# Two table splits of an expert loop computed on VectorE instead of GpSimd

## The chip, the cores and the metric

The kernel runs on one core of one Trainium2 chip. The metric is the device time of one execution in microseconds (us). The engines are named as in the profile: PE is TensorE's matrix multiplies, PEld its loads of weights, DVE is VectorE, ACT is ScalarE, POOL is GpSimd and SP is SyncE, which here only issues transfers.

## The reference, cut to what matters

The program is a whole network: two hybrid layers, a second block with attention and a recurrent branch, and at the end a layer of experts (`peer_ffn`), in which the change lies. Each of 512 tokens (1024 features) has 8 heads, and each head picks 16 of 16384 experts, by the best sums of two scores over 128 keys each. Expert e has a row of 1024 numbers in a first table `peer_u` and one in a second table `peer_v`.

```python
N_KEYS = 128; N_EXPERTS = N_KEYS * N_KEYS; PEER_HEADS = 8; PEER_TOPK = 16

def one_chunk(xc):                       # 128 tokens
    ...                                  # scores, top_s and eidx: the 16 best of each head
    gate = jax.nn.softmax(top_s, axis=-1)
    act = jax.nn.gelu(jnp.einsum('chkd,cd->chk', peer_u[eidx], xc))
    return jnp.einsum('chk,chkd->cd', (gate * act).astype(xc.dtype), peer_v[eidx])
```

## The kernel before

**Two ways for the tokens.** `peer` treats the four tiles of 128 tokens in two ways. Three of them (384 tokens) meet all 16384 experts: products of the tokens with the whole first table, gelu, multiplication by a matrix of gates that is zero where an expert was not chosen, and products with the whole second table. The fourth tile gathers its own experts: for each token one row of a table at a time, 128 times for the first table and 128 times for the second (`gathered`).

**The loop over the experts** (L2343) runs i from -7 to 127. A step takes 128 experts, and works on several of them at once: PE makes the products `u` of the first table for expert tile i+5 (24 matmuls, 384 columns each) and the products `acc` with the second table for tile i (18 matmuls, 512 columns each). For tiles 6 to 33 the first product was made earlier and is read back from DRAM (`xd`), so PE has the `u` part only from i = 29 on.

**High and low parts.** A table tile comes as 128x1024 fp32 (`raw`, 512 KB). `halves` (L2337) splits it into two fp32r tiles: ACT rounds it to the high part (`v<-raw` or `u<-raw`, a CAST), and another engine subtracts to get the low part (`v<-raw,v` or `u<-raw,u`, a TENSOR_TENSOR with two inputs in SBUF). PE makes three products for each pair of operands from them. There are 128 such tiles of the second table in the loop and 94 of the first one (from tile 34 on; the earlier ones are split elsewhere, and are not touched). The second table's tile is split two steps ahead of its use, for i+2, the first one's seven steps ahead, for i+7, and that is two steps before its product.

**What VectorE does in a step**, in its order: `x<-gq,x` and `x<-x,W` (gelu's second half and the gates, for tile i+3), `gq<-gq,x` (gelu's first half, tile i+4), `al<-x,ah` (low part of the gated activations, tile i+1), for even i the low part of the second table's tile, and then the fourth token tile's work. Up to i = 38 that is one step of its routing (top 16 and so on); after that it is about three gathered rows in a step, a dot product each (`pr<-gr,H`, L2577) while the first table is gathered, and a multiply-add each (`pr<-gr,gq,pr`, L2584) with the second.

**What GpSimd does in a step:** for odd i the low part of the second table's tile, from i = 27 on the low part of the first table's tile in every step, and from i = 39 on about three gathers (L2563, DMA_INDIRECT), each of which it issues itself.

**What sets the order.** In this loop PE, DVE, ACT and POOL execute in the order in which the program is written: `Core` wraps every engine, and its helper (L63) pins each instruction. So L63 is the line of nearly all of them, and rows are told apart by tile names. SP's loads are ordered by a scheduler. `raw` tiles come from a ring of 6 that a step takes two of; a load can start when the low part that read the slot before it is done. Gathered rows `gr` have a ring of 7 and are used 4 gathers after they are asked for (LAG). Tiles `u` and `v` have rings of 3, `ah` and `al` of 2.

Of the kernel before, what the change touches and what calls it, by code (L numbers as in the profile page):

```python
# [54 lines left out]
class Pinned:  # L55
    """An engine with its instructions in the order they are written in."""
# [9 lines left out]
class Core:  # L66
    """All engines so."""
# [7 lines left out]
class Feed:  # L75
    """Weights in the order of their use, 512 columns a tile, loaded ahead and split into two parts that one pass each carries."""

    def __init__(self, net, raw, split):
        self.net, self.nraw, self.nsplit = net, raw, split
        self.src, self.raws, self.tiles, self.over = [], [], {}, set()  # L80
        self.taken = self.dead = 0
        # another pool for what is loaded before weight number last
        self.more, self.last = None, 0

    def add(self, w, r0, c0, n, order=None, both=False):
        """1024 rows of n columns; returns the number of row tiles in a tile."""
        kt = min(KD, T // n)
        for rows in order or [range(k, k + kt) for k in range(0, KD, kt)]:
            self.src.append((w, r0 + rows[0] * P, rows[1] - rows[0], kt, c0, n, both))
        return kt  # L90
# [39 lines left out]
def part(gen, n):  # L130
    """The next n steps of a generator."""
    for _ in range(n):
        if next(gen, gen) is gen:
            return
        yield
# [7 lines left out]
def among(a, b, n):  # L143
    """A generator with n steps of another one after each of its own."""
    for _ in a:
        yield
        yield from part(b, n)


def weave(ticks, *work):  # L150
    """Steps of several generators in turn: (generator or (function, its argument), from, to, number of steps)."""
# [12 lines left out]
def tables():  # L164
    """Constants of shapes alone, [128, n] each: for all of the program, for block 1, for block 2."""
# [20 lines left out]
    # axial rotation, token major: [128, token tile, 64]  # L186
# [23 lines left out]
class Net:  # L210
# [34 lines left out]
    def row(self, ap, n, pool=None, tag=None):  # L245
        """A DRAM row of n on all partitions."""
# [4 lines left out]
    def wtile(self, w, r0, c0, n):  # L251
        """128 rows of a weight, split into two parts that one pass each carries."""
# [16 lines left out]
    def rstd(self, out, ss, n, eps=1e-6, nc=None):  # L269
        """out = (ss / n + eps) ** -0.5"""  # L270
# [12 lines left out]
    def defer(self, n, f, *x):  # L283
        """f, n steps of the projections later."""
# [12 lines left out]
    def unit_t(self, w, c0, x, evac, n=P, tok=slice(0, T)):  # L297
        """Eight steps to a block of columns of a product, transposed: evac(psum [n, tokens])."""
# [19 lines left out]
    def unit_n(self, w, r0, c0, x, evac, pairs=(0, 1), order=((0, 1), (2, 3), (4, 5), (6, 7))):  # L318
        """Eight steps to 256 columns of a product of each pair of token tiles: evac(pair, psum [tokens, 2, 256])."""
# [23 lines left out]
    def norm_pair(self, p, g, x, pool, s=1):  # L343
        """Two token tiles of X, normed, to columns of the transposed operand: staged, s steps for each stage."""
# [36 lines left out]
    def layer(self, l, S):  # L381
        """The layers of block 1 in two parts: the order of what meets the weights; the work. The heads run on a plan of
        ticks, 24 for a head of the first kind (M) and 12 for one of the second (B), and projections are woven in."""
# [13 lines left out]
        # ---- what follows the projections  # L397
# [49 lines left out]
        def rope(nm, b):  # L447
            """Rotated queries or keys of two heads, split as the products of scores take them."""
# [57 lines left out]
        # ---- the order of the weights  # L506
# [34 lines left out]
        # ---- the heads  # L541
# [5 lines left out]
        def pofs(d, i, t):  # L547
            """Column of key tile i, query tile t among the kept blocks."""
# [89 lines left out]
        def turned(n, src, k):  # L638
            """128 columns of a mixed output, transposed and split."""
# [67 lines left out]
        # ---- the work  # L707
# [69 lines left out]
    def norms(self, name, g, S):  # L777
        """What the staged norm of the two pairs of token tiles takes, and a new transposed operand."""
# [5 lines left out]
    def block1(self):  # L784
        tc, nc, a = self.tc, self.nc, self.a
        with ExitStack() as st:
            # on the way into block 2: the transposed operand, and until then X
# [8 lines left out]
            # the table of functions, before data is there  # L796
# [30 lines left out]
    def final_part(self, p, s, k):  # L827
        """X times the final gain, 256 columns of a pair of token tiles, and their sums of squares before and after."""
# [11 lines left out]
    def final_rest(self, p, xs, mod, bank, x, s, n0):  # L840
        """X = rms_norm(X, final_g) of two token tiles; normed once more, scaled and shifted per feature, to columns of
        the transposed operand. Staged, s steps for each stage."""
# [52 lines left out]
    def gates(self, l, ps, q, tl):  # L895
        """The gates of block 1 from their sums: staged."""
# [85 lines left out]
    def ahead(self, S):  # L982
        """What block 2 takes from its conditions and its context alone."""
# [16 lines left out]
    def block2_params(self, pool):  # L1000
# [16 lines left out]
        # lambda, the same on all partitions  # L1017
# [11 lines left out]
    def attn_params(self, cp):  # L1029
        nc, a = self.nc, self.a  # L1030
        self.load_tables(2, cp)
        # gains of q and k folded into the rotation
# [24 lines left out]
    def mods(self, pool):  # L1057
        """Modulation vectors: per feature columns, and rows for the two that gate a residual."""
# [48 lines left out]
    def modulated_xt(self, tiles, s1, sh, xh, xl, pool, bank, back=None, first=0, to=None):  # L1107
        """Normalised token tiles -> split transposed operand, scaled and shifted per feature, or as it is to DRAM."""
# [21 lines left out]
    def normed_of(self, src, pool, out=None):  # L1130
        """src / rms, in a tile of the pool or over src."""
# [10 lines left out]
    def block2(self):  # L1142
# [17 lines left out]
        # the operands of the projections again as places for others: of [128, T], high and low  # L1160
# [26 lines left out]
    def attention(self):  # L1187
        """Differential attention, a quarter (two heads) at a time; while the heads of one quarter run, the
        projections of the next are woven in. Yields once before x is needed, with the function that gives
        banks, and once before the last quarter, whose fill it is sent."""  # L1190
# [5 lines left out]
        with ExitStack() as left:  # L1196
# [8 lines left out]
            def loads():  # L1205
                """256 columns of the weight at a time, split in two: four tiles of two row tiles each."""
# [26 lines left out]
            def bank_of(i, xh, xl, b, evac, last=False):  # L1233
                """Projection i of two token tiles to 256 columns."""
# [14 lines left out]
            def headed(nm, q, o, rotate, last):  # L1249
                """Queries or keys of two token tiles: normed by heads, rotated, and split as the products take them."""  # L1250
# [52 lines left out]
            def ahead(u):  # L1303
                """What a quarter takes from the context: keys and values."""
# [37 lines left out]
            def scores(n):  # L1342
                """Products of queries and keys, and their exponentials: 4 ticks for each of a unit's four maps."""
# [28 lines left out]
            def turned(u):  # L1372
                """A quarter's outputs, transposed."""
# [16 lines left out]
            def outs(n, x):  # L1390
                """The difference of a unit's maps, transposed, and its product with the values."""
# [91 lines left out]
    def wblock(self):  # L1483
        """The next two row tiles of a block of 128 columns, of weights laid [128, block, 8, 128], split in two; others are asked for ahead."""
# [14 lines left out]
    def rwkv(self, hxh, hxl, hch, hcl, mmt2, bank2, lead):  # L1499
        """Delta-rule heads by chunks of 64 tokens, a block of 128 channels (two heads) at a time, both  # L1500
        directions together and in three groups: 4 chunks of context, then 4 and 4 of x. While the chain
        over the chunks of one group runs, the inverses of the next, the decays of the one after it and
        the projections of the next block are woven in."""
# [7 lines left out]
        with ExitStack() as st:  # L1511
# [12 lines left out]
            # what no chain takes: gives way to the work that fills the last ones  # L1524
# [21 lines left out]
            def proj(b, dst, both=True):  # L1546
                """Shifted channels of block b, of context and x."""
# [18 lines left out]
            def block(ct, o):  # L1566
                """Projections, unit keys, bonus of a block of channels."""
# [9 lines left out]
                # unit keys, times -1/2  # L1577
# [25 lines left out]
            def tail(o):  # L1603
                """Bonus and values of a block of channels."""
                k, r, v, ct = o["k"], o["r"], o["v"], o["ct"]
                # bonus
                rk = tl([P, T], "rk")
                nc.vector.scalar_tensor_tensor(rk, r, self.rk_[:, ct:ct + 1], k[:, C:], op0=ALU.mult, op1=ALU.mult)
                # values, token major
# [15 lines left out]
            def pairs(j):  # L1625
                """The first of the group's two pairs of chunks, for each direction."""
                return ((0, 0), (2, 4), (4, 2))[j]

            def decays(o, g):
                """Decays and rates of a group, and its keys and receptances with the decays on them."""  # L1630
# [33 lines left out]
                # slots of a chunk pair: k even, b even, b odd, k odd; r even, kk even, kk odd, r odd  # L1664
# [15 lines left out]
            def products(o, g):  # L1680
                """Products within the chunks of a group, in both directions."""
# [4 lines left out]
                for d in range(2):  # L1686
# [17 lines left out]
                    # keys and rates, token major, stacked as the values are  # L1704
# [8 lines left out]
            def values(o, g):  # L1713
                """Values over and under zeros, for what is found of the rates."""
# [8 lines left out]
            def newton(x):  # L1723
# [16 lines left out]
                def keep(ps, Z):  # L1740
                    """Into the diagonal blocks that the steps of the chain take."""
# [9 lines left out]
            def chain(o, g):  # L1751
                """The state over the four chunks of a group, and what the receptances read of it."""
# [81 lines left out]
            def gate(b):  # L1834
                """A block of the merge gates, to DRAM: work that fills the tensor engine."""
# [22 lines left out]
            def branch_in(src, ks, at):  # L1858
                """Rows of a branch's outputs, split."""
# [20 lines left out]
            def branch(b, ks, at, evac, *src):  # L1880
                """A block of a branch's product."""
# [16 lines left out]
            def gated_b(b, ps, g, f):  # L1898
                """Of the branches merged by their gates all but what the last block of the second one brings."""
# [4 lines left out]
            # where no operand stands any more when the second branch is under way  # L1904
# [757 lines left out]
```

## Time and profile before

| what | value |
|---|---|
| median of 3 runs | 4966.08 us |
| lowest and highest run | 4948.15 and 4974.35 us |
| span of the profiled execution | 4986.3 us |
| PE busy in it | 4530.2 us, 91% |
| DVE busy | 3463.8 us, 69% |
| ACT busy | 1993.8 us, 40% |
| POOL busy | 2156.0 us, 43% |

The profiled execution is known by its span alone, 4986.3 us from its first to its last instruction; that is 20 us (0.4%) above the median of the timed runs. A busy share is a mean over the whole network. The loop over the experts takes the stretch from about 3870 us to the end, and shares of that stretch are read from views of it. An instruction's time in a row begins when its engine takes it up; an engine that has started an instruction but cannot go on shows a long instruction, not an idle gap.

### The profile page before, as it was taken

What the parts mean: (1) busy time and instruction counts of PE and PEld (TensorE: products, weight loads), DVE (VectorE), ACT (ScalarE), POOL (GpSimd) and SP (SyncE); (2) the same over time, 40 slices, a digit from 0 to 9 for tenths busy, and PEclk for the clock granted to TensorE, in tenths of its full rate; (3) what the DMA queues carried; (4) which work ended last, traced back from release to release, by engine and by line L of the source; (5) the groups of instructions that cost most, each with busy time, mean ns of one, the idle gap of its engine ahead of it and who ended that gap; (6) DMA issues with size and microseconds to landing.
All of it is one profiled execution on the core that took longest, in us unless ns stands there. A gap on an engine that the chain in (4) does not pass through costs nothing. (4 is left out here: it accounts for less than half of the span.)

```text
span 4986.3 us, 78323 instructions
## 1 busy us (share of the span) xinstructions
PE 4530.2 (91%) x29167; PEld 3864.4 (78%) x29167; DVE 3463.8 (69%) x6705; ACT 1993.8 (40%) x4288; POOL 2156.0 (43%) x1715
## 2 busy tenths in 40 slices
PE   8999999999998998888898889889799889988987
PEld 6789897888888886677776767768677678877776
DVE  4654234655656654677777877668753989999999
ACT  3444334443325554344444444433222444333333
POOL 3324443324434332322232333144433247888886
PEclk8999999999999999788788888999678999999999
DMA  4234333235653211000000001462344447887886
GB/s 128 72 86 133 96 115 98 69 89 157 189 186 112 55 46 42 19 21 18 20 21 23 23 26 36 134 213 92 104 125 153 158 160 274 294 289 278 289 291 230
DMA packets 435687, 618.46 MB, mean 124 GB/s; under 512 B 32596, under 2 KB 318436, under 8 KB 435176
## 3 DMA queue, kind: packets, MB, share of 16 engines
q1 hardware_dynamic: 392104, 469.87, 30.0%
q0 software_dynamic: 36864, 134.23, 7.8%
q10 hardware_dynamic: 6336, 9.35, 0.6%
q8 instruction: 229, 3.75, 0.3%
q14 instruction: 154, 1.26, 0.1%
HBM read 549.36 MB, written 48.24 MB: 120 GB/s over the span
## 5 line engine op out<-in xcount | busy, mean ns | idle before, releaser
L63 POOL TENSOR_TENSOR wlo<-wraw,whi 128x512 fp32r<-128x512 f32 x451 | 614.9, 1369 | 897.3 <-ACT whi L63 850.6
L63 ACT CAST whi<-wraw 128x512 fp32r<-128x512 f32 x572 | 347.3, 617 | 564.4 <-PE mm L63 369.8
L63 PE MATMUL acc<-v,ah 128*128 128x512 f32 x1536 | 444.7, 414 | 4.3 <-ACT ah L63 4.3
L1495 POOL TENSOR_TENSOR wbl<-wblk,wbh 128x256 fp32r<-128x256 f32 (+1 forms) x184 | 148.3, 806 | 615.4 <-ACT wbh L1494 362.9
L63 PE MATMUL u<-hph,u 128*128 128x384 f32 x1504 | 400.6, 338 | 4.5 <-ACT x L63 4.5
L63 PE MATMUL mm<-whi,u 128*128 128x256 f32 x2048 | 377.2, 285 | 4.5 <-ACT u L63 2.7
L63 PE MATMUL acc<-v,al 128*128 128x512 f32 x768 | 264.2, 427 | 113.1 <-DVE al L63 112.8
L63 PEld LDWEIGHTS acc<-v,ah 128*128 128x128 f32 x1536 | 309.0, 202 | 68.0 <-ACT ah L63 4.6
L63 PE MATMUL mm<-xh,whi 128*128 128x512 f32 (+2 forms) x880 | 342.8, 390 | 8.0 <-ACT r L63 4.6
L63 PE MATMUL mm<-xh,wlo 128*128 128x512 f32 (+2 forms) x880 | 328.9, 374 | 0.0
L63 PEld LDWEIGHTS mm<-whi,u 128*128 128x128 f32 x2048 | 323.4, 193 | 6.5 <-ACT u L63 3.3
L63 PE MATMUL mm<-xl,whi 128*128 128x512 f32 (+2 forms) x880 | 328.4, 373 | 0.0
L63 POOL TENSOR_TENSOR u<-raw,u 128x1024 fp32r<-128x1024 f32 x94 | 273.3, 2908 | 81.0 <-ACT u L63 80.8
L63 ACT ACTIVATE gq<-gq 128x384 f32<-128x384 f32 x128 | 67.1, 524 | 595.4 <-DVE gq L63 595.4
L63 PE MATMUL mm<-wlo,u 128*128 128x256 f32 x1024 | 291.6, 285 | 5.0 <-POOL wlo L63 4.6
L63 PEld LDWEIGHTS acc<-v,al 128*128 128x128 f32 x768 | 151.5, 205 | 169.4 <-DVE al L63 140.4
L63 PEld LDWEIGHTS u<-hph,u 128*128 128x128 f32 x1504 | 275.4, 189 | 9.1 <-ACT x L63 4.9
L63 DVE SCALAR_TENSOR_TENSOR x<-gq,x 128x384 f32<-128x384 f32 x128 | 264.6, 2067 | 12.9 <-ACT gq L63 12.2
L63 POOL TENSOR_TENSOR v<-raw,v 128x1024 fp32r<-128x1024 f32 x64 | 195.1, 3048 | 171.7 <-ACT v L63 159.6
L63 PE MATMUL u<-hpl,u 128*128 128x384 f32 x752 | 253.5, 337 | 0.0
L63 PE MATMUL mm<-whi,xh 128*128 128x256 f32 x768 | 236.0, 307 | 0.0
L63 PE MATMUL mm<-whi,xl 128*128 128x256 f32 x768 | 219.5, 286 | 0.1
(608 smaller groups left out, 13232.8 us busy)
## 6 DMA issues: line engine op xcount, KB each, us to landing
raw<-in_ut_dram SPq DMA_DIRECT2D x128, 512.0 KB
raw<-in_peer_v_dram SPq DMA_DIRECT2D x128, 512.0 KB
wraw<-in_w_in_dram SPq DMA_DIRECT2D x184, 256.0 KB
wraw<-in_w_down_dram SPq DMA_DIRECT2D x160, 256.0 KB
wraw<-in_w_up_dram SPq DMA_DIRECT2D x152, 256.0 KB
mraw<-in_w_mod_dram SPq DMA_DIRECT2D x96, 256.0 KB
wg<-stage SPq DMA_DIRECT2D x12, 2048.0 KB
W<-wg SPq DMA_DIRECT2D x32, 768.0 KB
```

What stands on the lines that cost most here:

```text
L63: return lambda *a, **k: self.tc.keep_in_program_order(f(*a, **k))
L1495: (nc.vector if self.wn > WN and n % 2 else nc.gpsimd).tensor_tensor(lo, raw, hi.bitcast(F32), op=ALU.subtract)
```

## The change

Both calls of `halves` in the loop name VectorE as the engine that subtracts. For the second table that moves 64 of 128 low parts, those of odd i, and for the first table all 94. The computation, the tiles, their rings and all other instructions stay. The diff also empties docstrings and comments in the file, without moving a line; those hunks are left out.

```diff
@@ -2385,9 +2385,9 @@
                 if 0 <= i + 2 < P:
-                    halves(i + 2, "v", gp, k.gpsimd if i % 2 else k.vector)
+                    halves(i + 2, "v", gp, k.vector)
                 if NA <= i + 7 < P:
-                    halves(i + 7, "u", wp, k.gpsimd)
+                    halves(i + 7, "u", wp, k.vector)
```

First place: VectorE, two steps of the loop while rows of the first table are gathered, before the change. `gr` are gathered rows; the second step here has no low part of a table at all.

```order
 L63 TENSOR_TENSOR v_43796<-raw_43600,v_43795 128x1024
 L2577 ISA pr_43288,act_43287<-gr_43673,H 128x1024
...
 L63 SCALAR_TENSOR_TENSOR x_43786<-gq_43788,x_43786 128x384
 L63 TENSOR_TENSOR x_43786<-x_43786,W_43450 128x384
 L63 SCALAR_TENSOR_TENSOR gq_43864<-gq_43864,x_43862 128x384
 L63 TENSOR_TENSOR al_43868<-x_43632,ah_43867 128x384
 L2577 ISA pr_43288,act_43287<-gr_43749,H 128x1024
```

The same two steps on VectorE after the change:

```order
 L63 TENSOR_TENSOR v_43796<-raw_43600,v_43795 128x1024
 L63 TENSOR_TENSOR u_43800<-raw_43602,u_43799 128x1024
 L2577 ISA pr_43288,act_43287<-gr_43673,H 128x1024
...
 L63 SCALAR_TENSOR_TENSOR x_43786<-gq_43788,x_43786 128x384
 L63 TENSOR_TENSOR x_43786<-x_43786,W_43450 128x384
 L63 SCALAR_TENSOR_TENSOR gq_43864<-gq_43864,x_43862 128x384
 L63 TENSOR_TENSOR al_43868<-x_43632,ah_43867 128x384
 L63 TENSOR_TENSOR v_43872<-raw_43676,v_43871 128x1024
 L63 TENSOR_TENSOR u_43876<-raw_43678,u_43875 128x1024
 L2577 ISA pr_43288,act_43287<-gr_43749,H 128x1024
```

Each step now has both low parts between `al` and the first dot product.

Second place: GpSimd in the same steps, the difference of its order from before to after.

```order
-L63 TENSOR_TENSOR u_43800<-raw_43602,u_43799 128x1024
 L2563 DMA gr_43821<-in_peer_u_dram,ei_43211 128x1024
 L2563 DMA gr_43824<-in_peer_u_dram,ei_43211 128x1024
 L2563 DMA gr_43827<-in_peer_u_dram,ei_43211 128x1024
-L63 TENSOR_TENSOR v_43872<-raw_43676,v_43871 128x1024
-L63 TENSOR_TENSOR u_43876<-raw_43678,u_43875 128x1024
 L2563 DMA gr_43897<-in_peer_u_dram,ei_43211 128x1024
 L2563 DMA gr_43900<-in_peer_u_dram,ei_43211 128x1024
```

Three subtractions in two steps are gone from GpSimd, and only the gathers are left on it here. The order on PE and ACT is the same before and after. On SP a few loads trade places before i = 27, a read of `xd` with the load of `peer_v` next to it; the later loads keep their order.

## Rows read from the trace of the kernel before

**Rows 1.** The page, the chain of work that ended last, shares by line.

```profile
DVE x L63 5%; DVE pr L2584 3%; DVE pr L2577 2%; PE acc L2535 2%; PE acc L2536 2%; DVE gq L63 1%; PE acc L63 1%; DVE al L63 1%; DVE v L63 1%; PE u L63 1%; PE u L267 1%; PE u L266 1%; PE u L265 1%; DVE sel L2489 0%; DVE pz L2479 0%
```

**Rows 2.** Busy us by stretch: PE, PEld, DVE, ACT, POOL; then clock, DMA share, GB/s.

```profile
3900.00:4000.00 100.00, 82.55 (x324) 64.08 (x324) 97.25 (x220) 41.88 (x73) 26.65 (x11) 0.93 0.52 170
4054.00:4131.00 77.00, 76.62 (x381) 69.70 (x382) 61.05 (x56) 37.72 (x60) 37.30 (x15) 0.98 0.47 154
4205.00:4546.00 341.00, 305.44 (x1443) 269.61 (x1442) 337.26 (x372) 126.60 (x204) 279.05 (x159) 0.94 0.82 291
...
4296.00:4304.00 8.00, 8.00 (x43) 7.31 (x41) 7.90 (x8) 1.39 (x2) 7.35 (x4) 1.00 1.02 419
```

**Rows 3.** Timeline of VectorE, two steps: start us, us, engine, line, operation.

```profile
4281.38 2.73 DVE L63 SCALAR_TENSOR_TENSOR x<-gq,x 128x384 f32<-128x384 f32 x1
...
4289.52 2.73 DVE L63 SCALAR_TENSOR_TENSOR x<-gq,x 128x384 f32<-128x384 f32 x1
...
4293.99 1.22 DVE L63 TENSOR_TENSOR v<-raw,v 128x1024 fp32r<-128x1024 f32 x1
4295.12 1.22 DVE L2577 CUSTOM_DVE_ANT_0 pr<-gr,H 128x1024 f32<-128x1024 f32 x1
...
4297.65 3.29 DVE L2577 CUSTOM_DVE_ANT_0 pr<-gr,H 128x1024 f32<-128x1024 f32 x1
...
4300.88 2.75 DVE L63 SCALAR_TENSOR_TENSOR x<-gq,x 128x384 f32<-128x384 f32 x1
```

**Rows 4.** Timeline of GpSimd, the same two steps.

```profile
4280.34 3.36 POOL L63 TENSOR_TENSOR u<-raw,u 128x1024 fp32r<-128x1024 f32 x1
...
4286.57 1.30 POOL L2563 DMA_INDIRECT gr<-in_peer_u_dram,ei  x1 [0.31 <-issue]
4289.31 2.52 POOL L63 TENSOR_TENSOR u<-raw,u 128x1024 fp32r<-128x1024 f32 x1 [1.44 <-ACT u L63]
...
4296.52 3.35 POOL L63 TENSOR_TENSOR v<-raw,v 128x1024 fp32r<-128x1024 f32 x1 [0.50 <-ACT v L63]
```

**Rows 5.** Timeline of VectorE while the second table is gathered: `x` at three places.

```profile
4698.50 2.74 DVE L63 SCALAR_TENSOR_TENSOR x<-gq,x 128x384 f32<-128x384 f32 x1
...
4718.29 2.75 DVE L63 SCALAR_TENSOR_TENSOR x<-gq,x 128x384 f32<-128x384 f32 x1
...
4937.19 0.55 DVE L63 SCALAR_TENSOR_TENSOR x<-gq,x 128x384 f32<-128x384 f32 x1
```

**Rows 6.** VectorE's groups, 4143.7 to 4969 us: busy us, mean ns, idle before.

```profile
L2584 DVE SCALAR_TENSOR_TENSOR pr<-gr,gq,pr 128x1024 f32<-128x1024 f32 x127 | 211.5, 1665 | 4.3 <-DMA gr<-in_peer_v_dram,ei 1.4
L63 DVE SCALAR_TENSOR_TENSOR x<-gq,x 128x384 f32<-128x384 f32 x83 | 210.2, 2533 | 0.0
L2577 DVE CUSTOM_DVE_ANT_0 pr<-gr,H 128x1024 f32<-128x1024 f32 x126 | 195.6, 1552 | 3.0
```

**Rows 7.** GpSimd's groups, 4143.7 to 4969 us.

```profile
L63 POOL TENSOR_TENSOR u<-raw,u 128x1024 fp32r<-128x1024 f32 x80 | 237.2, 2965 | 57.5 <-ACT u L63 57.3
...
L63 POOL TENSOR_TENSOR v<-raw,v 128x1024 fp32r<-128x1024 f32 x43 | 142.9, 3323 | 29.6 <-ACT v L63 21.2 <-issue 8.4
```

**Rows 8.** GpSimd's groups, 3870 to 4054 us.

```profile
L63 POOL TENSOR_TENSOR v<-raw,v 128x1024 fp32r<-128x1024 f32 x16 | 40.0, 2498 | 121.2 <-ACT v L63 117.5 <-DVE v L63 3.6
...
L63 POOL TENSOR_TENSOR u<-raw,u 128x1024 fp32r<-128x1024 f32 x3 | 7.8, 2584 | 4.5 <-ACT u L63 4.5
```

**Rows 9.** The chain that ended last, two pieces of it: start us, us, what.

```profile
4059.46 4.17 PE u L63 x24
4063.62 4.08 PE acc L63 x18
```

**Rows 10.** Timeline of PE, a wait and what follows it.

```profile
4207.91 0.72 PE L63 MATMUL acc<-v,al 128*128 128x512 f32 x2 [2.72 <-DVE al L63]
4208.47 1.71 PE L63 MATMUL acc<-v,ah 128*128 128x512 f32 x4
```

**Rows 11.** All gathers of the second table: lowest, median and highest ns of one.

```profile
L2563 POOL DMA_INDIRECT gr<-in_peer_v_dram,ei x128: 958/1098/2006, 4540.3 to 4951.7; - x128
```

## The prediction

> **What bounds the kernel now.** I read the chain that ended last first, then busy time by stretch, then the timelines of VectorE and GpSimd over the same two steps. The chain's shares [rows 1] are led by VectorE's work in the expert loop: `x`, and `pr` of both gatherings. By stretch [rows 2] the loop has three parts. From 3900 to 4000 us VectorE is busy 97.25 of 100 us and PE 82.55. From 4054 to 4131 us PE is busy 76.62 of 77 us and VectorE 61.05: PE is the bound. From 4205 us to nearly the end VectorE is busy 337.26 of 341 us, PE 305.44 at a clock of 0.94, and the transfers run at 291 GB/s with a share of 0.82. So VectorE sets the pace before 4054 us and after 4143.7 us, where the first dot products are under way.
>
> But a busy VectorE isn't a working one. `x` takes 2.73 to 2.75 us in rows 3 and 0.55 us at 4937.19 us [rows 5], with the same shape; `pr` takes 3.29 us at 4297.65 us and 1.22 us at 4295.12 us. Each long one meets a subtraction on GpSimd [rows 4]: the `u` of 4289.31 us ends at 4291.83 us, and the `x` begun at 4289.52 us ends 0.42 us later, about its own length less what overlaps. The `v` of 4296.52 us starts beside a `pr` and takes 3.35 us; the next `pr` has to wait for it. At 4937.19 us, with no subtraction on GpSimd, `x` is short. The gathers that GpSimd issues (1.30 us at 4286.57 us) lie beside instructions of VectorE that keep their 1.22 us. So VectorE stands still while GpSimd subtracts, and not while it issues gathers.
>
> The Trainium skill (SBUF — State Buffer, section "SBUF: two separate sides") says that VectorE, with two inputs in SBUF, and GpSimd take turns on one port pair, each for a whole instruction; the trace agrees (3.29 us in place of 1.22). A rule of it speaks against this change: Perfetto Trace Analysis, section "Optimizing Scalar/DVE Operations", says that offloading between these two might not help, because of that port. By it the sum below would be zero; its rival has a chance of its own.
>
> **The change part by part.**
>
> *What goes.* In the two steps from 4281.38 to 4300.88 us (19.50 us) GpSimd subtracts three times, and VectorE loses (2.73 - 0.55) + (3.29 - 1.22) + (2.75 - 0.55) = 6.45 us, 2.15 us for each [rows 3, 5]. Over the whole main stretch [rows 6]: `x` 83 x (2.53 - 0.55) = 164 us; dot products 126 x (1.55 - 1.22) = 42 us; multiply-adds 127 x (1.665 - 1.27) = 50 us, where 1.27 is the dot's 1.22 plus a sixth of the 0.29 us by which two steps are longer there (4718.29 - 4698.50 = 19.79 us [rows 5]). Together 256 us, against 80 + 43 = 123 subtractions [rows 7]: 2.08 us each. I take 2.1 us.
>
> *What comes.* The same subtraction on VectorE, for even i, is 1.22 us long, and the next instruction starts 1.13 us after it [rows 3]. So one that moves gives VectorE 2.1 - 1.13 = 0.97 us.
>
> *Main stretch.* 123 x 0.97 = 119 us, if VectorE stays the bound. Two steps then take 19.50 - 3 x 0.97 = 16.6 us, and 16.9 us with multiply-adds. The next one late is PE: `u` 4.17 us and `acc` 4.08 us at full clock [rows 9], so 16.5 us for two steps. The two are nearly equal, and this is all that the change can bring: PE's floor for the stretch is 80 x 8.25 + 6 x 4.08 = 684 us (six last steps without `u`) of 825 us, a gain of 141 us at most.
>
> *Early part.* Before 4054 us 16 + 3 = 19 subtractions move [rows 8], worth at most 19 x 0.97 = 18 us. VectorE isn't quite always the bound there; I take 15 us. The 16 between 4054 and 4143.7 us (158 in all less 123 and 19) bring nothing: PE sets the pace, and VectorE's 61 of 77 us leave room for them.
>
> *Waits that the change adds.* On VectorE the low parts wait for ACT's high parts, with the dot products and the next `x` queued behind. GpSimd takes up the `v` of 4296.52 us right after ACT's cast; VectorE's place for it is behind the `x` of 4300.88 us and three more instructions. So it has over 4 us in hand, and this wait costs nothing as long as ACT is a step ahead; if it were not, a whole cast would be lost per step. `al`, for which PE waits, stands before the low parts and isn't delayed by them. The slots of `raw` come free by VectorE's subtraction in place of GpSimd's; SP's loads behind have about two steps to land. SP's few exchanged loads before i = 27 change no load's size, and I cost them at nothing: each trades one place with a neighbour, and these steps use 0.52 of the transfers' time. On GpSimd the gathers are no longer queued behind subtractions and can only start earlier.
>
> *Sum.* 119 + 15 = 134 us. For two engines with nearly equal cycles, where each waits for the other's jitter, I take 4 us off. So 130 us: 4986.3 - 130 = 4856 us for the profiled span. The span is 20 us above the median of the runs; the gain lies in a loop whose steps repeat, so I take it off the median: 4966 - 130 = **4836 us**.
>
> **The rivals.**
>
> *Transfers become the bound.* Each step moves 291 GB/s x 9.75 us = 2.84 MB; at 8.3 us that is 342 GB/s, and the share would be 0.82 x 9.75 / 8.3 = 0.96. For it: the present bursts fill the queues only now and then. Against it: from 4296 to 4304 us 419 GB/s were moved at a full share [rows 2], and loads come more evenly when all low parts are in one place. If the mean share can't pass 0.90, a step takes 8.9 us, and with 9.8 us before, 80 x 0.9 + 15 = 87 us are gained: 4879 us.
>
> *PE becomes the bound at less than its full clock.* After a wait of 2.72 us four matmuls take 1.71 us [rows 10] where 4 x 4.08 / 18 = 0.91 us is usual: half speed, that is 1.2 for 2.4 GHz. If PE's waits for `al` get short but stay, with the mean clock at 0.94 [rows 2], a step takes 8.25 / 0.94 = 8.8 us: 80 x 1.0 + 15 = 95 us, 4871 us. Against it: from 4054 to 4131 us PE ran without waits at 0.98.
>
> *Gathers starve (slower).* GpSimd writes what the gathers need while VectorE now runs two-input instructions without a pause. An issue is 1.1 us in the median and 2.01 at most [rows 11], with 0.31 us between two [rows 4]. Three of them fill a step of 8.3 us from 2.5 us each, and the kernel gets slower than before from 2.95 us each. Had each to wait out two subtractions, 1.1 + 2.26 + 0.3 = 3.7 us, a step would take 11 us: 85 x 1.2 - 15 = 87 us slower, 5053 us. Against it: in rows 4 gathers were issued beside a VectorE that never paused.
>
> [...]
>
> *One for one.* VectorE would lose as much by the low parts as by standing still; 4966 us. Rows 3 speak against it (1.13 against 2.15 us).
>
> *The long `x` has another cause* that stays, and the low parts come on top: 142 x 1.13 = 160 us, 5126 us.
>
> **How the numbers follow.** Forecast 0.73, transfers 0.10, PE's clock 0.09, gathers 0.04, one for one 0.02, another cause 0.02. About 0.5% (25 us) is what a measurement of this kernel can tell from no change. The first three are faster by more than that: 0.92. Within it lies one for one: 0.02. Slower are the last and the starved gathers: 0.06. The range goes from 141 + 18 us (PE's floor and all of the early part), 4807 us, to a little above the transfers' case, 4888 us, since the timed runs spread by 26 us.
>
> **What would show it.** `x` at 0.55 us and `pr` at 1.22 us throughout; 128 `v` and 94 `u` low parts on VectorE at 1.22 us; two steps of 16.5 to 17 us; PE near 95 of 100 us or more at a clock near 1; gathers still near 1.1 us. I am wrong if `x` stays long, if an issue of a gather passes 2.5 us, or if VectorE or ACT waits for `raw` or `gr` step after step.

## Result and profile after

The changed kernel takes 4816.41 us in the median (4 runs, 4805.59 to 4831.27) against 4969.55 us for the kernel before (4 runs, 4948.15 to 4974.35): ratio 0.9696, 95% interval 0.9662 to 0.9731, so 3% faster, by 153 us. The forecast was 4836 us, with a range from 4807 to 4888 us.

The profiled execution spans 4816.9 us. First VectorE over two steps, where [rows 3] showed the kernel before (timeline: start us, us, engine, line, operation):

```profile
4273.14 0.55 DVE L63 SCALAR_TENSOR_TENSOR x<-gq,x 128x384 f32<-128x384 f32 x1
...
4275.44 1.22 DVE L63 TENSOR_TENSOR v<-raw,v 128x1024 fp32r<-128x1024 f32 x1
4276.58 1.22 DVE L63 TENSOR_TENSOR u<-raw,u 128x1024 fp32r<-128x1024 f32 x1
4277.72 1.22 DVE L2577 CUSTOM_DVE_ANT_0 pr<-gr,H 128x1024 f32<-128x1024 f32 x1
...
4281.39 0.55 DVE L63 SCALAR_TENSOR_TENSOR x<-gq,x 128x384 f32<-128x384 f32 x1
...
4289.65 0.55 DVE L63 SCALAR_TENSOR_TENSOR x<-gq,x 128x384 f32<-128x384 f32 x1
```

`x` is 0.55 us in each of these steps instead of 2.73 us, and no `pr` of the loop is long (1.23 and 1.29 us at most). The two low parts stand behind each other at 1.14 us. A step takes 8.26 us, two 16.51 us, where two took 19.50 us.

GpSimd in the second of these steps, for [rows 4]:

```profile
4279.21 1.80 POOL L2563 DMA_INDIRECT gr<-in_peer_u_dram,ei  x1 [3.80 <-DVE act L2577]
4281.31 0.96 POOL L2563 DMA_INDIRECT gr<-in_peer_u_dram,ei  x1 [0.30 <-issue]
4282.58 1.09 POOL L2563 DMA_INDIRECT gr<-in_peer_u_dram,ei  x1 [0.31 <-issue]
```

Only gathers are left, and GpSimd now waits 3.8 us in a step until VectorE has used a gathered row.

Busy time by stretch after the change, for [rows 2] (PE, PEld, DVE, ACT, POOL; then clock, DMA share, GB/s):

```profile
3848.70:4000.00 151.30, 132.90 (x522) 102.50 (x523) 146.83 (x365) 69.42 (x119) 4.48 (x2) 0.94 0.54 173
4000.00:4095.00 95.00, 94.77 (x485) 86.61 (x484) 72.77 (x101) 46.07 (x73) 13.61 (x9) 1.00 0.60 204
4095.00:4440.00 345.00, 345.00 (x1758) 315.50 (x1757) 339.50 (x502) 160.92 (x245) 161.88 (x126) 1.00 0.95 341
4440.00:4627.00 187.00, 187.00 (x954) 170.91 (x953) 183.92 (x205) 88.17 (x140) 90.22 (x68) 1.00 0.94 334
4627.00:4795.00 168.00, 162.41 (x809) 146.28 (x808) 165.87 (x181) 71.30 (x116) 74.46 (x57) 0.99 0.89 317
```

From 4000 to 4627 us PE is busy without a gap, at a clock of 1.00 (2.4 GHz); before, it was busy 305 of 341 us at 0.94. VectorE is busy 339.5 of 345 us beside it: the two are nearly even. The chain says the same. Its shares by engine and line, from the page (compare [rows 1]), and pieces of it in order of time:

```profile
PE 21%; DVE 7%; issue 1%; DMA 0%; POOL 0%; ACT 0%; DVEq 0%; POOLq 0%; ACTq 0%
PE acc L63 8%; PE u L63 6%; PE acc L2535 2%; PE acc L2536 2%; DVE pr L2584 1%; PE u L267 1%; PE u L266 1%; PE u L265 1%; DVE v L63 1%; DVE gq L63 1%; DVE al L63 0%; DVE u L63 0%; DVE x L63 0%; DVE sel L2489 0%; DVE pz L2479 0%
...
4619.36 4.16 PE u L63 x24
4623.53 4.09 PE acc L63 x18
4632.18 1.30 DVE pr L2584
```

The chain runs through PE's steps of 8.25 us until 4627 us. Then it passes to VectorE, whose step with multiply-adds is 8.4 us: from there on VectorE is late, and PE waits.

**Where the time went.** Three marks cut the loop: the first `acc` matmul, the first dot product and the last multiply-add. Their starts, in the profile's groups by tile:

```profile
L63 PE MATMUL acc<-v,ah x1536: 387/389/797, 3848.7 to 4807.6; 128*128 128x512 f32 x192
L2577 DVE CUSTOM_DVE_ANT_0 pr<-gr,H x128: 1207/1224/1230, 4095.0 to 4439.7; 128x1024 f32<-128x1024 f32 x128
L2584 DVE SCALAR_TENSOR_TENSOR pr<-gr,gq,pr x127: 1270/1285/1286, 4447.6 to 4795.0; 128x1024 f32<-128x1024 f32 x127
```

The same rows of all profiles give this table (us). The main part is from the first dot product to the last multiply-add; the last column is the time before the loop.

| kernel | to the first dot | main part | to the end | whole loop | before the loop |
|---|---|---|---|---|---|
| before | 263.3 | 823.6 | 23.4 | 1110.3 | 3876.0 |
| changed | 246.3 | 700.0 | 21.9 | 968.2 | 3848.7 |
| e_u (first table only) | 257.1 | 737.4 | 24.0 | 1018.5 | 3872.0 |
| e_v (second table only) | 252.2 | 773.0 | 19.8 | 1045.0 | 3865.5 |
| e_allpool | 274.3 | 868.1 | 19.8 | 1162.2 | 3875.8 |
| e_none | 214.3 | 691.4 | 20.7 | 926.4 | 3866.9 |
| e_tt | 281.2 | 941.9 | 19.7 | 1242.8 | 3879.3 |
| e_copy | 258.2 | 837.1 | 19.7 | 1115.0 | 3872.5 |
| e_set | 246.1 | 700.6 | 21.3 | 968.0 | 3871.3 |

The loop gained 142 us: 17 us before the first dot product and 124 us in the main part. The remaining 27 us between the two profiled spans lie before the loop. The profiles above have the same code there (but for one fill in e_tt, e_copy and e_set) and start the loop between 3849 and 3879 us, so 27 us lie within what that part varies by and can't be put down to the change.

**What VectorE's long instructions add up to.** Both ends of the main part are instructions of VectorE, so the work and the waits of VectorE fill it. For each row of VectorE in that part I take the busy time less the number of instructions times their length in the changed kernel, which has no long ones there (`x` 0.552, `x<-x,W` 0.849, `gq` 0.551, `al` 0.549, low parts 1.217, dot products 1.222, multiply-adds 1.283 us). The sum is what VectorE loses beside GpSimd. Three rows of the kernel before, two of e_u and two of e_v, which hold most of it:

```profile
L63 DVE SCALAR_TENSOR_TENSOR x<-gq,x 128x384 f32<-128x384 f32 x84 | 210.8, 2509 | 0.0
L2584 DVE SCALAR_TENSOR_TENSOR pr<-gr,gq,pr 128x1024 f32<-128x1024 f32 x126 | 208.2, 1652 | 4.3 <-DMA gr<-in_peer_v_dram,ei 1.4
L2577 DVE CUSTOM_DVE_ANT_0 pr<-gr,H 128x1024 f32<-128x1024 f32 x128 | 198.1, 1547 | 6.3 <-DMA gr<-in_peer_u_dram,ei 3.2
...
L2584 DVE SCALAR_TENSOR_TENSOR pr<-gr,gq,pr 128x1024 f32<-128x1024 f32 x126 | 201.9, 1602 | 3.0
L2577 DVE CUSTOM_DVE_ANT_0 pr<-gr,H 128x1024 f32<-128x1024 f32 x128 | 193.8, 1514 | 4.3 <-DMA gr<-in_peer_u_dram,ei 1.4
...
L2584 DVE SCALAR_TENSOR_TENSOR pr<-gr,gq,pr 128x1024 f32<-128x1024 f32 x126 | 237.9, 1888 | 3.6 <-DMA gr<-in_peer_v_dram,ei 0.7
L2577 DVE CUSTOM_DVE_ANT_0 pr<-gr,H 128x1024 f32<-128x1024 f32 x128 | 233.2, 1822 | 6.5 <-DMA gr<-in_peer_u_dram,ei 3.6
```

| kernel | GpSimd's work in the main part, besides gathers | VectorE loses (us) | for each |
|---|---|---|---|
| before | 124 subtractions | 262.7 | 2.12 |
| e_u | 43 subtractions | 85.2 | 1.98 |
| e_v | 80 subtractions | 163.5 | 2.04 |
| e_allpool | 166 subtractions | 352.1 | 2.12 |
| e_tt | 121 scratch subtractions | 240.8 | 1.99 |
| e_copy | 121 copies | 136.1 | 1.12 |
| e_set | 242 fills | 0.5 | 0.00 |

The change gives VectorE 262.7 us back and costs it 123 x 1.14 = 140 us: 122 us, and the main part gained 123.6 us.

### The profile page after: what moved, and what is told of

Its sections match the earlier page's. It is cut to its first block, busy times and chain, and to the rows that moved or that the text cites. A ratio compares the mean times of both kernels' runs of the same rounds, so it can differ in the third digit from the quotient of the medians.

```text
span 4816.9 us, 78238 instructions
## 1 busy us (share of the span) xinstructions
PE 4456.5 (93%) x29167; PEld 3820.2 (79%) x29167; DVE 3323.6 (69%) x6863; ACT 2003.1 (42%) x4288; POOL 1726.0 (36%) x1557
## 5 line engine op out<-in xcount | busy, mean ns | idle before, releaser
L63 PE MATMUL acc<-v,ah 128*128 128x512 f32 x1536 | 419.7, 396 | 4.3 <-ACT ah L63 4.3
L63 PEld LDWEIGHTS acc<-v,ah 128*128 128x128 f32 x1536 | 292.5, 191 | 60.2 <-ACT ah L63 4.6
L63 PE MATMUL acc<-v,al 128*128 128x512 f32 x768 | 243.4, 399 | 26.5 <-DVE al L63 26.5
L2563 POOL DMA_INDIRECT gr<-in_peer_u_dram,ei x128 | 165.0, 1289 | 251.7 <-DVE act L2577 158.4
L2563 POOL DMA_INDIRECT gr<-in_peer_v_dram,ei x128 | 170.0, 1328 | 183.4 <-DVE pr L2584 152.8
L63 PE MATMUL mm<-wlo,xh 128*128 128x256 f32 x768 | 219.4, 286 | 0.0
L63 DVE TENSOR_TENSOR wlo<-wraw,whi 128x512 fp32r<-128x512 f32 x121 | 103.0, 852 | 146.0 <-ACT whi L63 140.4
L63 PEld LDWEIGHTS mm<-wlo,u 128*128 128x128 f32 x1024 | 198.3, 194 | 5.5 <-POOL wlo L63 4.7
```

Source lines behind the costliest of these rows:

```text
L63: return lambda *a, **k: self.tc.keep_in_program_order(f(*a, **k))
L2563: tc.keep_in_program_order(nc.gpsimd.indirect_dma_start(out=r, out_offset=None, in_=w, in_offset=bass.IndirectOffsetOnAxis(ap=ei[:, i:i + ...
```

## The experiments

Theory: a GpSimd instruction that reads SBUF makes VectorE's instructions with two inputs stand still for about its own length; on VectorE the subtraction costs 1.13 us. Rivals: the gain comes from GpSimd's queue, in which gathers stood behind subtractions; or after the change VectorE still sets the pace; or transfers or PE's clock stop the gain. The kernel before took 4967.62 us beside the first four, 4980.45 us beside the next four and 4976.96 us beside the last three. e_tt, e_copy and e_light are one run each.

**e_u: only the first table's low parts move.**

```diff
-                    halves(i + 2, "v", gp, k.vector)
+                    halves(i + 2, "v", gp, k.gpsimd if i % 2 else k.vector)
                 if NA <= i + 7 < P:
                     halves(i + 7, "u", wp, k.vector)
```

> Only the 94 low parts of the first table move to VectorE; the second table's odd ones stay on GpSimd. Theory (a subtraction on GpSimd holds VectorE up for 2.1 us, one on VectorE costs 1.13 us): two steps in the main stretch take 19.5 - 2 x 0.97 = 17.6 us, more than PE's 16.5, so VectorE stays the bound and the whole gain shows: 80 x 0.97 + 3 = 81 us, about 4888 us against 4970, ratio 0.984. Rival (the gain comes from GpSimd's queue, where gathers stand behind subtractions, and not from VectorE): the queue still has a subtraction in every second step, less than half of the gain, 4910 us or more, and long x instructions gone where GpSimd still subtracts.

Measured: 4881.98 us, ratio 0.982 (0.9793 to 0.9847). By the table the main part gains 86.2 us, 1.08 us for each of 80 low parts. The theory's time, and not the rival's.

**e_v: only the second table's odd low parts move.**

```diff
                     halves(i + 2, "v", gp, k.vector)
                 if NA <= i + 7 < P:
-                    halves(i + 7, "u", wp, k.vector)
+                    halves(i + 7, "u", wp, k.gpsimd)
```

> Only the 64 odd low parts of the second table move to VectorE; all 94 of the first table stay on GpSimd. Theory: two steps take 19.5 - 0.97 = 18.5 us; 43 x 0.97 + 15 in the early part = 57 us, about 4913 us against 4970, ratio 0.9885. Both parts add up: e_u and e_v together should gain what the whole change gains (142 us within the loop by the profile), or somewhat more, since with the whole change PE's 16.5 us becomes a floor. Rival (GpSimd's queue): little or nothing, 4950 us or more, since a subtraction stays in front of the gathers in every step.

Measured: 4913.51 us, ratio 0.9891 (0.9863 to 0.9919). Main part 50.6 us, 1.18 us for each of 43, with a subtraction left in front of the gathers in every step. So the queue is not it. Both single moves together gain 86.2 + 50.6 = 136.8 us in the main part, and the whole change only 123.6 us. The 13 us stand in the table of what VectorE loses: with both kinds of subtraction on GpSimd it is 262.7 us, with each kind alone 85.2 + 163.5 = 248.7 us, 14 us less. So each single move also saves what only the two kinds together cost, and adding the two gains counts that twice. Why the two kinds together cost more, no run here shows.

**e_allpool: the other way, all low parts on GpSimd.**

```diff
-                    halves(i + 2, "v", gp, k.gpsimd if i % 2 else k.vector)
+                    halves(i + 2, "v", gp, k.gpsimd)
                 if NA <= i + 7 < P:
                     halves(i + 7, "u", wp, k.gpsimd)
```

> The other direction: all low parts of both tables on GpSimd, so 64 more than before the change. Theory: each of the 64 costs 2.1 us of holding up in place of 1.13 us on VectorE; 43 in the main stretch and most of the early ones: 50 to 62 us slower, about 5025 us. If moving work off the busy VectorE were what counts: 64 x 1.13 = 72 us faster, 4900 us.

Measured: 5037.98 us, ratio 1.014 (1.011 to 1.017). 43 more subtractions on GpSimd lengthen the main part by 44.5 us, 1.03 us each: VectorE got less to do, and the kernel got slower. The whole loop is 52 us longer, within the 50 to 62 us; the medians of the timed runs are 70 us apart.

**e_none: no low parts at all.** PE reads the high part in the low part's place.

```diff
-                hi, lo = (pool.tile([P, D], F32R, tag=tag + x, name=self.uid(tag), bufs=3) for x in "hl")
-                q[tag, i] = hi, lo
+                hi = pool.tile([P, D], F32R, tag=tag + "h", name=self.uid(tag), bufs=3)
+                q[tag, i] = hi, hi
                 k.scalar.copy(hi, raw)
-                eng.tensor_tensor(lo, raw, hi.bitcast(F32), op=ALU.subtract)
...
```

> Leaves the low parts of both tables out: no subtraction on any engine in the loop, and PE reads the high parts in their place, with all its matmuls. VectorE's step falls from 8.26 to about 6.0 us. Theory (with the change PE is the bound at 8.25 us a step from 4000 to 4627 us): next to nothing there; the early part gains up to 29 x 1.13 = 33 us, down to PE's 4.08 us a step, and the late part some 10 us: 4770 to 4790 us against 4816. Rival (VectorE still sets the pace after the change): 80 x 2.26 = 180 us less, about 4636 us.

Measured: 4794.07 us (4764.27 to 4795.98), just above the theory's 4770 to 4790 us. The main part in one stretch, here and in the changed kernel (columns as above):

```profile
4081.20:4772.60 691.40, 691.40 (x3517) 631.72 (x3516) 509.90 (x722) 323.21 (x502) 322.12 (x249) 1.00 0.92 338
...
4095.00:4795.00 700.00, 694.41 (x3517) 632.69 (x3516) 689.29 (x886) 320.39 (x501) 326.56 (x249) 1.00 0.93 334
```

With 165 low parts fewer (84 of the second table, 81 of the first), VectorE is busy for 509.9 in place of 689.3 us, and the main part falls only from 700.0 to 691.4 us, in which PE has no gap. So 691 us is PE's floor. In the changed kernel the two are within 8.6 us of each other, and VectorE is still the longer: it waits for other engines for 1.9 us in all in the main part, and PE waits for `al` for 5.6 us, all after 4627 us. But the rival's 180 us are not there: at most 8.6 us are left in the main part for a further change to VectorE. Before the first dot product 32 us go: there VectorE still sets the pace.

**e_tt: GpSimd's subtractions back, without their work.** The changed kernel, with a subtraction on GpSimd that nothing waits for at each of the 158 places.

```diff
+            scr = gp.tile([P, D], F16, tag="scr", name="scr")
+            nc.gpsimd.memset(scr, 0.0)
...
                     halves(i + 2, "v", gp, k.vector)
+                    if i % 2:
+                        k.gpsimd.tensor_tensor(scr, scr, scr, op=ALU.subtract)
...
                     halves(i + 7, "u", wp, k.vector)
+                    k.gpsimd.tensor_tensor(scr, scr, scr, op=ALU.subtract)
```

> The changed kernel, with a subtraction on GpSimd of the same number of elements (128x1024, fp16, a scratch tile with itself) at each of the 158 places that the change freed; nothing waits for it, and it waits for nothing. Theory (holding up): VectorE pays both prices, its own 1.13 us and about 2.1 us: two steps 16.5 + 3 x 2.1 = 22.8 us, 5110 to 5140 us; x and pr long again. Rival (GpSimd's queue, or its waits for ACT and raw): GpSimd is as busy as before the change, so the time is at most that of before, 4970 us, and VectorE's instructions stay short.

Measured: 5123.84 us, slower than the kernel before by 143 us. VectorE and GpSimd in one step (two timelines):

```profile
4299.31 0.84 DVE L63 TENSOR_TENSOR x<-x,W 128x384 f32<-128x384 f32 x1
4300.07 0.55 DVE L63 SCALAR_TENSOR_TENSOR gq<-gq,x 128x384 f32<-128x384 f32 x1
4300.54 2.78 DVE L63 TENSOR_TENSOR al<-x,ah 128x384 fp32r<-128x384 f32 x1
4303.24 1.21 DVE L63 TENSOR_TENSOR v<-raw,v 128x1024 fp32r<-128x1024 f32 x1
...
4300.99 1.90 POOL L63 TENSOR_TENSOR scr<-scr 128x1024 f16<-128x1024 f16 x1
```

`al` takes 2.78 us in place of 0.55 us while GpSimd works for 1.90 us on a tile that nobody else uses. The main part is 241.9 us longer than the changed kernel's. GpSimd's scratch work there:

```profile
L63 POOL TENSOR_TENSOR scr<-scr 128x1024 f16<-128x1024 f16 x121 | 241.8, 1998 | 4.6
```

That is 2.00 us for each of 121, as long as they run. Nothing waits for this tile, and VectorE waits for other engines for only 0.8 us in the main part; its long instructions make 240.8 us by the table. So it is the running of the one beside the other that costs.

**e_copy: a copy with one input in the same places instead.**

```diff
+                        k.gpsimd.tensor_copy(scr, scr)
```

> As the kernel with the scratch subtraction, but a copy on GpSimd with one input (128x1024, fp16, in place). Theory: if any reading of SBUF by GpSimd holds VectorE's two-input instructions up, each copy costs VectorE as long as the copy runs; with 1 us each two steps take 19.5 us and the time is about 4940 us. If only the length of GpSimd's work beside VectorE counted, its cost would be the same share of its length as the subtraction's. If a copy does not hold VectorE up: 4816 us.

Measured: 4989.26 us, 50 us above the 4940 us of the theory. That estimate took 1 us for each and left the early part out, which is 26 us of it (14 in the main part, 12 before the first dot product); of the rest, 24 us lie before the loop in the profile, where the two kernels have the same instructions but for one fill. The group by tile, and the same copies in the main part:

```profile
L63 POOL COPY scr<-scr x158: 1037/1053/1921, 3858.5 to 4955.0; 128x1024 f16<-128x1024 f16 x158
...
L63 POOL COPY scr<-scr 128x1024 f16<-128x1024 f16 x121 | 138.8, 1148 | 2.9
```

The main part is 137.1 us longer than the changed kernel's, and 121 copies take GpSimd 138.8 us in it. One input is enough, and VectorE loses GpSimd's length.

**e_set: two fills in each place, which read nothing.**

```diff
+                        [k.gpsimd.memset(scr, 0.0) for _ in range(2)]
```

> As the kernel with the scratch subtraction, but two fills on GpSimd (128x1024, fp16, no input) at each of the 158 places. GpSimd's queue is filled, and it reads nothing from SBUF. Theory (two-input instructions of VectorE are held up only by a GpSimd that reads): 4816 us, within 10 us, and x at 0.55 us. Rival (GpSimd's queue in front of the gathers): 4850 to 4970 us. If writing alone holds VectorE up too: x is long, 4900 us or more.

Measured: 4831.57 us, ratio 0.9702 (0.9674 to 0.9731), the changed kernel's own within the interval. GpSimd and VectorE in one stretch:

```profile
4302.24 4.00 POOL L63 MEMSET scr<- 128x1024 f16 x4
...
4303.89 0.55 DVE L63 SCALAR_TENSOR_TENSOR x<-gq,x 128x384 f32<-128x384 f32 x1
4304.48 0.87 DVE L63 TENSOR_TENSOR x<-x,W 128x384 f32<-128x384 f32 x1
4305.27 0.55 DVE L63 SCALAR_TENSOR_TENSOR gq<-gq,x 128x384 f32<-128x384 f32 x1
4305.74 0.55 DVE L63 TENSOR_TENSOR al<-x,ah 128x384 fp32r<-128x384 f32 x1
```

Four fills of 4.00 us together lie beside VectorE's instructions, and none is longer for it. GpSimd's queue is fuller in front of the gathers, and the main part stays at 700.6 us. With e_tt, e_copy and e_set the question is settled for these instructions: reading SBUF on GpSimd is what stops VectorE; writing alone and a full queue are not. GpSimd's length alone is not it either: the two fills of a place are as long as one subtraction of e_tt.

**e_light: where the transfers end.** e_none, with one of PE's three passes left in the loop.

```diff
-                        for l, r in ((uh, hh), (uh, hl), (ul, hh)):
+                        for l, r in ((uh, hh),):
...
-                    for l, r in ((ah, vh), (ah, vl), (al, vh)):
+                    for l, r in ((ah, vh),):
...
```

> Leaves the low parts of both tables out and with them two of PE's three passes in the loop, so PE's step falls to about 2.8 us and VectorE's to about 6.0 us; the transfers are all there. It shows where the transfers end: with the changed kernel they run at 341 GB/s with a share of 0.95. If they can give 419 GB/s throughout: 2.84 MB in 6.8 us a step, 80 x 1.45 = 116 us less there and the early part down to VectorE's 4 us a step, about 4660 us. If 355 GB/s is the end: 8.0 us a step, 4770 us, so the changed kernel would be within 0.25 us a step of it.

Measured: 4615.48 us, 45 us below the 4660 us: the part before the first dot product fell from 246.3 to 168.8 us, by 77 us where I had taken 40. A stretch of 400 us, with the columns as above:

```profile
4100.00:4500.00 400.00, 242.81 (x816) 198.00 (x817) 350.82 (x512) 217.36 (x354) 222.85 (x178) 0.78 1.02 417
```

The transfers gave 417 GB/s for 400 us. The changed kernel needs 341 GB/s, 82% of that. By this rate a step can't be shorter than 2.84 MB / 417 GB/s = 6.8 us; PE's is 8.25 us.

**e_after, e_eq and e_more: further in the same direction.** e_eq also moves 16 multiplications (fp16) of the routing to VectorE, 4 in the loop and 12 before it. e_more moves, besides, the low parts of the first table's first 34 tiles and GpSimd's half of the `hot` products, all before the loop. e_after is the changed kernel beside them.

```diff
-            nc.gpsimd.tensor_tensor(eq, eq, sf[:, j:8:2, :, None].to_broadcast(sh), op=ALU.mult)
+            nc.vector.tensor_tensor(eq, eq, sf[:, j:8:2, :, None].to_broadcast(sh), op=ALU.mult)
...
-                        uh, ul = split(a["ut"][i], "u", nc.gpsimd)
+                        uh, ul = split(a["ut"][i], "u", nc.vector)
...
-                (nc.gpsimd if n.start % 16 else nc.vector).tensor_tensor(hot[3], hot[0], bc(3), op=ALU.mult)
+                nc.vector.tensor_tensor(hot[3], hot[0], bc(3), op=ALU.mult)
```

> The changed kernel once more, beside the two kernels that go further, on the same chip: 4816 us, ratio 0.970 to the kernel before.

> The changed kernel, and the 16 multiplications of eq by sf in the routing (fp16, 128x1024) on VectorE instead of GpSimd too, 4 of them in the expert loop, 12 before it in a stretch (3400 to 3540 us) in which VectorE is busy 137 of 140 us. On GpSimd one takes 1.9 us before the loop and 2.4 us in it. Theory (holding up): each holds VectorE up for about 1.9 us or has it wait for the product, and costs it 0.6 us on its own: 16 x 1.3 = 21 us at most where VectorE is the bound, so 4795 to 4805 us. Rival (one for one, the work only changes place): 4816 us. Other rival (the product on VectorE is much slower than GpSimd's because of its operand that is repeated inside a row): slower than 4816 us.

> As the kernel with the multiplications of eq on VectorE, and also the low parts of the first 34 tiles of the first table, which are split before the loop, and the half of the hot products that GpSimd computes in the stretch in which the matrix of gates is built (24 of 48). Theory: in the routing's stretch up to 3540 us VectorE is the bound, and about 8 low parts lie there, 8 x 1 = 8 us; from 3540 to 3815 us PE is busy all the time and VectorE about half of it, so nothing comes of the rest: 4785 to 4800 us. Rival (in the stretch of the gates PE waits for VectorE, which then has more to do in its order): 4816 us or more.

Measured: e_after 4827.20 us, ratio 0.9707 (0.9687 to 0.9728); e_eq 4840.48 us, 0.9722 (0.9698 to 0.9746); e_more 4832.79 us, 0.9704 (0.9687 to 0.9722). No difference that can be measured: my expectations of 11 to 21 us more (e_eq) and 16 to 31 us more (e_more) were a miss. The price was wrong for a start; the group of e_eq's products before the loop:

```profile
L2486 DVE TENSOR_TENSOR eq<-eq,sf x12: 1201/1217/3415, 3447.8 to 3574.9; 128x1024 f16<-128x1024 f16 x12
```

1.22 us on VectorE, not the 0.6 us that I took from the comparison of the same shape. And on GpSimd only a part of these products had stopped VectorE. In the changed kernel, before the loop and then in it:

```profile
3410.38 4.23 DVE L2489 TENSOR_REDUCE sel<-eq 128x64 f32<-128x1024 f16 x2
...
3410.54 1.92 POOL L2486 TENSOR_TENSOR eq<-eq,sf 128x1024 f16<-128x1024 f16 x1 [1.39 <-DVE eq L2485]
...
3923.36 2.27 DVE L63 SCALAR_TENSOR_TENSOR x<-gq,x 128x384 f32<-128x384 f32 x1
3925.66 2.43 DVE L63 TENSOR_TENSOR x<-x,W 128x384 f32<-128x384 f32 x1
...
3922.92 4.48 POOL L63 TENSOR_TENSOR eq<-eq,sf 128x1024 f16<-128x1024 f16 x2 [87.56 <-DVE eq L63]
```

Before the loop two reductions on VectorE took 4.23 us, 2.12 us each, beside a product on GpSimd; the loop's shortest is 2.12 us, so they go on. In the loop two products made `x` and `x<-x,W` 3.3 us longer together. Of the 12 products before the loop the six that meet a `pz` stop it (last section), for about 1.7 us each: by these rows, as an estimate, 10 us are saved there and 12 x 1.1 = 14 us spent, so nothing is won. Of the rest of e_more, the stretch of the gates, only the total was measured. So none of these versions beats the changed kernel.

## Why the prediction was right

**What bounds the kernel.** A VectorE that is 99% busy but stands still for a part of it: shown by e_tt, e_copy and e_set, with nothing changed but what GpSimd does beside it. The Trainium skill (SBUF — State Buffer, section "SBUF: two separate sides") restricts the turn-taking for VectorE's two-input instructions to a GpSimd instruction that reads SBUF; the copy (held) and the fill (not held) agree with it.

**The price of a subtraction on GpSimd** was right: 2.1 us forecast, 2.12 us by the sum of VectorE's long instructions. The sum of the prediction left out `al` and `x<-x,W`, which are held now and then too, but they are 8.1 and 1.7 us of 262.7. VectorE's own price, 1.13 us, is in the trace after (1.14 us). The 1.11 us for each that e_u and e_v together show (136.8 / 123) is not the net price of the whole change: it counts twice the 14 us that the two kinds of subtraction cost only together.

**Main stretch: 119 us forecast, 124 us measured.** The 4 us that I took off for the coupling were not lost: VectorE waits for 1.9 us in the main part. That PE would be the next one late, with 16.5 us for two steps, was right, and the two are as close as forecast: 700.0 us by VectorE, and PE's floor is 691 us (e_none), where I had 684 us.

**Early part: 15 us forecast, 17 us measured.** The size is right, its place not quite. The prediction had nothing gained after 4054 us; PE's first `u` comes 151.5 us after the first `acc` (4000.2 us) in place of 163.1 us (4039.1 us), 11.6 us earlier, and the other 5.4 us fall between that `u` and the first dot product.

**The waits that I costed at nothing** stayed so: VectorE waited 3.4 us in all, in 8 waits, for ACT's high parts of the second table, and never for `raw`. One wait grew that the prediction doesn't name: VectorE's `al` for ACT's `ah`, from 7.6 to 16.5 us over the loop, all but 0.7 us of it before the first dot product.

**The sum.** 130 us forecast; the loop gained 142 us in the profiles, and the timed runs differ by 153 us (134 to 168 us by the ratio's interval). Where the 20 us lie by which the profiled span of before exceeded the median, the profiles don't show: its 3876.0 us before the loop are among the longer ones, 3849 to 3879 us. Subtracting from the median came nearer than subtracting from the span.

**The rivals.** *Transfers:* not the bound; 341 of 417 GB/s. The share came out as computed (0.95 at 341 GB/s, 0.96 forecast for 342), but it says little about what is left: e_light has 1.02 at 417 GB/s, so a share of 0.95 still had a fifth in reserve. *PE's clock:* with the waits gone it is 1.00, not 0.94. *Starved gathers:* an issue is 1.08 and 1.05 us in the median of the two tables, though the first of a burst takes 1.80 us; GpSimd waits for VectorE, not the other way. One issue of 256 took 4.53 us (at 4443.98 us, where the second table begins), more than the 2.5 us that I had named as a sign of being wrong; the others stayed below 2 us, and VectorE waited for no gathered row. *One for one:* the rule in Perfetto Trace Analysis of the Trainium skill, section "Optimizing Scalar/DVE Operations", that moving work between these two might not help, did not hold in the loop, where 2.12 us were exchanged for 1.14 us; e_eq shows a place where nothing came of it. *Another cause:* excluded by e_tt.

## What to carry to other kernels

When VectorE is the bound, look for instructions that are several times longer than their like and lay GpSimd's timeline beside them: work on GpSimd that reads SBUF is then not free, but costs VectorE's instructions with two inputs about its full length. Compare what it costs with what the instruction would take on VectorE; here it was 2.12 against 1.14 us, and e_allpool shows that giving VectorE less to do can make the kernel slower. Before you add the gains up, work out the next engine's floor for the same step: this change brought its full price and ended 8.6 us above PE's floor, so the next one of its kind would bring next to nothing. And gains of two halves, measured one by one, need not add up (137 against 124 us here): sum what the bound engine loses in each version instead.

## What the runs showed of the hardware that was not expected

- A fill on GpSimd (0.95 us, fp16 128x1024) costs VectorE nothing measurable: 316 of them in e_set, with the loop at 968.0 against 968.2 us.
- It is not only instructions with two tensors that are stopped. In the changed kernel, a `TENSOR_SCALAR` of 64 elements with one tensor, 0.20 us in the loop, lasted until GpSimd had finished (two timelines), and all six of its kind before the loop took 1.78 to 2.25 us:

```profile
3407.42 1.78 DVE L2479 TENSOR_SCALAR pz<-pa 128x64 f32<-128x64 f16 x1
...
3407.24 1.91 POOL L2486 TENSOR_TENSOR eq<-eq,sf 128x1024 f16<-128x1024 f16 x1 [2.06 <-DVE eq L2485]
```

  Why this one is stopped and the reductions beside the next product are not, no run here tells apart.
- The loads and gathers together reached 417 GB/s over 400 us, with the mean busy share at 1.02.
